# Channel shuffle on one core: the second load goes to ScalarE's queue, and the 16 KB tile moves from the last place to the third

## The chip, the core and the metric

The kernel runs on one core of a Trainium2 chip. The time is in device microseconds (us): the median of three runs, 316.16 us (316.13 to 316.22). One further view is the profile of a single execution, which took 316.22 us; its traced span is 314.4 us, and the 1.8 us between lie around the span. Of the engines only three matter here: SyncE (SP) and ScalarE (ACT), which issue the transfers between the chip's memory (HBM) and the core's on-chip memory (SBUF), and VectorE (DVE), which copies. The transfers are carried out by the core's 16 DMA engines.

## The reference

```python
batch, h, w, c = 16, 64, 64, 256      # x, float32; groups = 8
channels_per_group = c // groups      # 32
x = x.reshape(batch, h, w, groups, channels_per_group)
x = x.transpose(0, 1, 2, 4, 3)
x = x.reshape(batch, h, w, c)
```

Each of the 65,536 rows of 256 floats is permuted in the same way: read as an 8 x 32 matrix, it is written transposed. There is no arithmetic. 67.11 MB are read and 67.11 MB are written.

## The kernel before

The rows lie one behind the other in memory, 1 KB each. The kernel cuts them into tiles. A tile of "q KB" gives each of the 128 partitions q whole rows that lie one behind the other, so each partition's part is one contiguous piece of q KB in HBM and in SBUF; the tile holds q x 128 KB.

The list `_SLOTS` (line 12) gives the sizes and the order. An entry is one buffer's filling, and an entry with several numbers is one buffer that is loaded, copied and stored in several pieces, side by side in the buffer. Before the change it reads: one buffer with a 4 KB and an 8 KB piece, one with 28 KB, twelve with 38 KB, one with 16 KB. They sum to 512 KB a partition. All buffers have the size of the biggest entry, 38 KB.

There are two input buffers (`_IN_BUFS`) and three output buffers (`_OUT_BUFS`), taken in turn. For each entry the loop does three things. The loads of all its pieces are issued by SP (line 55). Then, piece by piece, VectorE copies from the input to the output buffer, and the copy's access pattern does the transposition (line 57), and ACT issues the store (line 61).

The order on each engine is the order of the program (the schedule is manual). What sets the pace between engines is the buffers. SP issues the first loads of the first two entries without waiting. The load of entry n waits until the copies of entry n-2 have all read their input buffer; SP's queue holds nothing else. A copy waits for its own load, and for the stores of entry n-3 to have left its output buffer. A store waits for its copy. SP's loads and ACT's stores stand in two DMA queues, called q1 and q10 in the profile, which the same 16 DMA engines serve. At the end SP waits for the last stores (line 94).

## Time and profile before

| What | Value |
|---|---|
| median of 3 runs | 316.16 us (316.13 to 316.22) |
| profiled execution, its own time | 316.22 us |
| its span | 314.4 us |
| VectorE busy | 119.0 us (38%), 16 copies |
| mean DMA rate over the span | 427 GB/s (134.22 MB) |
| copy of a 38 KB tile | 8.79 us (mean of 12) |
| copy of 28, 16, 8, 4 KB | 6.57, 3.87, 2.02, 1.09 us |
| load of a 38 KB tile, issue to landing | 37.0 us (median) |
| store of a 38 KB tile, issue to landing | 42.6 us (median) |
| load of 4, 8, 28, 16 KB, issue to landing | 3.3, 5.4, 14.7, 30.4 us |
| store of 4, 8, 28, 16 KB, issue to landing | 14.3, 25.0, 30.9, 15.2 us |

The busy times are per engine, over the span. The time from issue to landing runs from the instruction that issues a transfer to the last of its bytes; it includes the waiting behind earlier transfers of the same queue and the sharing of the DMA engines with the other queue, so it isn't the time that the transfer would take alone. In a timeline line the first number is the start in us from the span's start, the second the duration, and the square brackets hold the engine's idle time just before and what ended it.

### The profile page before, as it was taken

What the parts mean: (1) busy time and instruction counts of PE and PEld (TensorE: products, weight loads), DVE (VectorE), ACT (ScalarE), POOL (GpSimd) and SP (SyncE); (2) the same over time, 40 slices, a digit from 0 to 9 for tenths busy, and PEclk for the clock granted to TensorE, in tenths of its full rate; (3) what the DMA queues carried; (4) which work ended last, traced back from release to release, by engine and by line L of the source; (5) the groups of instructions that cost most, each with busy time, mean ns of one, the idle gap of its engine ahead of it and who ended that gap; (6) DMA issues with size and microseconds to landing.
All of it is one profiled execution on the core that took longest, in us unless ns stands there. A gap on an engine that the chain in (4) does not pass through costs nothing.

```text
span 314.4 us, 132 instructions
## 1 busy us (share of the span) xinstructions
DVE 119.0 (38%) x16; POOL 0.2 (0%) x4
## 2 busy tenths in 40 slices
DVE  2081907309109109019028028037046055065400
POOL 0000000000000000000000000000000000000000
DMA  7999999999999999999999999999999999999997
GB/s 317 405 441 416 435 416 483 401 465 406 450 421 446 426 436 436 401 470 396 475 396 475 396 470 401 470 401 470 401 450 421 446 426 436 436 417 450 429 421 321
DMA packets 4608, 134.22 MB, mean 427 GB/s; under 512 B 512, under 2 KB 512, under 8 KB 768
## 3 DMA queue, kind: packets, MB, share of 16 engines
q1 hardware_dynamic: 2304, 67.11, 49.8%
q10 hardware_dynamic: 2304, 67.11, 49.4%
HBM read 67.11 MB, written 67.11 MB: 427 GB/s over the span
## 4 chain that ended last, share of the span: by engine, by line
DMA 76%; DVE 19%; issue 0%; SPq 0%; DVEq 0%
DMA in_tile<-in_x_dram 76%; DVE out_tile L57 19%; SPq L55 0%; DVEq L57 0%
## 5 line engine op out<-in xcount | busy, mean ns | idle before, releaser
L57 DVE COPY out_tile<-in_tile 128x9728 f32<-128x9728 f32 (+4 forms) x16 | 119.0, 7440 | 179.4 <-DMA in_tile<-in_x_dram 179.4
L80 POOL MEMSET const-uint8-127<- 128x1 uint8 x1 | 0.1, 103 | 0.0
L80 POOL MEMSET const-bfloat16-1.0<- 128x1 bf16 x1 | 0.1, 102 | 0.0
L80 POOL MEMSET const-float32-1.0<- 128x1 f32 x1 | 0.1, 100 | 0.0
L80 POOL MEMSET const-float32-0.0<- 128x1 f32 x1 | 0.1, 99 | 0.2 <-issue 0.2
## 6 DMA issues: line engine op xcount, KB each, us to landing
in_tile<-in_x_dram SPq DMA_DIRECT2D x12, 4864.0 KB, 37.0
out_dram<-out_tile ACTq DMA_DIRECT2D x12, 4864.0 KB, 42.6
in_tile<-in_x_dram SPq DMA_DIRECT2D x1, 3584.0 KB, 14.7
out_dram<-out_tile ACTq DMA_DIRECT2D x1, 3584.0 KB, 30.9
in_tile<-in_x_dram SPq DMA_DIRECT2D x1, 2048.0 KB, 30.4
out_dram<-out_tile ACTq DMA_DIRECT2D x1, 2048.0 KB, 15.2
in_tile<-in_x_dram SPq DMA_DIRECT2D x1, 1024.0 KB, 5.4
out_dram<-out_tile ACTq DMA_DIRECT2D x1, 1024.0 KB, 25.0
```

Source lines behind the costliest of these rows:

```text
L57: nc.vector.tensor_copy(out=out_tile[:, cols].rearrange("p (i j g) -> p i j g", j=CPG, g=G), in_=in_tile[:, cols].rearrange("p (i g j) -> ...
L80: nc = _bacc.Bacc("TRN2", target_bir_lowering=False, num_devices=1)
```

## The change

Two things change. In the list of sizes the 16 KB tile is no longer an entry of its own at the end: it is the third piece of the first entry, behind 4 and 8 KB. The list has 14 entries instead of 15, with the same 16 pieces, and the last entry is now a 38 KB tile. The load of the 8 KB piece is issued by ACT, and all other loads by SP as before. The order on SP is now 4, 16, 28 KB, then twelve times 38 KB; on ACT it is the 8 KB load and then the stores of 4, 8, 16, 28 KB and twelve of 38 KB; on VectorE the copies run in the order of the stores. The first 38 KB load now waits for the copies of three pieces, the last of them the 16 KB one.

```diff
-_SLOTS = [[4, 8], [28]] + [[38]] * 12 + [[16]]
+_SLOTS = [[4, 8, 16], [28]] + [[38]] * 12
...
         for q, start, cols in pieces:
-            nc.sync.dma_start(out=in_tile[:, cols], in_=rows(x_flat, start, q))
+
+            queue = nc.scalar if q == 8 else nc.sync
+            queue.dma_start(out=in_tile[:, cols], in_=rows(x_flat, start, q))
         for q, start, cols in pieces:
             nc.vector.tensor_copy(
```

## The prediction

> **What bounds the kernel now.** I read the page first: the busy shares, the slices, the DMA queues.

> ```profile
> DVE 119.0 (38%) x16; POOL 0.2 (0%) x4
> ...
> DMA  7999999999999999999999999999999999999997
> ...
> q1 hardware_dynamic: 2304, 67.11, 49.8%
> q10 hardware_dynamic: 2304, 67.11, 49.4%
> ```

> The only compute engine is idle 62% of the time. The DMA engines are busy in every slice, and the loads (queue 1, issued by SP) and the stores (queue 10, issued by ACT) together fill 99.2% of their span. So the question for any edit is: does it make the DMA engines idle for longer or shorter, or does it change the bytes per microsecond? The chain of waits, read alone, would mislead: it puts 19% on VectorE, but while it walks through a copy another load and a store are moving. The timeline gives the rate. A copy that waits for its load starts as the load lands, so copy starts are load landings:

> ```profile
> 4.06 1.09 DVE L57 COPY out_tile<-in_tile 128x1024 f32<-128x1024 f32 x1 [4.06 <-DMA in_tile<-in_x_dram]
> 6.61 2.02 DVE L57 COPY out_tile<-in_tile 128x2048 f32<-128x2048 f32 x1 [1.46 <-DMA in_tile<-in_x_dram]
> 16.36 6.57 DVE L57 COPY out_tile<-in_tile 128x7168 f32<-128x7168 f32 x1 [7.73 <-DMA in_tile<-in_x_dram]
> ...
> 71.31 8.75 DVE L57 COPY out_tile<-in_tile 128x9728 f32<-128x9728 f32 x1 [13.40 <-DMA in_tile<-in_x_dram]
> ...
> 278.19 8.73 DVE L57 COPY out_tile<-in_tile 128x9728 f32<-128x9728 f32 x1 [14.21 <-DMA in_tile<-in_x_dram]
> 294.54 3.87 DVE L57 COPY out_tile<-in_tile 128x4096 f32<-128x4096 f32 x1 [7.62 <-DMA in_tile<-in_x_dram]
> ```

> From 71.31 to 278.19 nine 38 KB tiles land, and as many stores leave: 206.88 / 9 = 22.99 us for 2 x 38 = 76 KB a partition, or 0.3025 us per KB a partition. I call 1 KB a partition one unit. The whole kernel moves 512 units in and 512 out: 1024 x 0.3025 = 309.8 us of the 314.4 us span. Only 4.6 us lie outside. Of them 2.85 stand before and in the first landing (4.06 minus 4 x 0.3025 = 1.21), and 0.75 behind the last store's landing (298.45 issued, 15.2 to land, 313.65; span end 314.4). About 1 us is lost on the way. The head and one dip show in the table of stretches (columns: stretch, its length, DVE, POOL, clock, DMA share, GB/s):

> ```profile
> 1.50:2.00 0.50, 0.00 (x0) 0.00 (x0) 1.00 0.74 90
> 2.00:2.50 0.50, 0.00 (x0) 0.00 (x0) 1.00 0.45 164
> 2.50:5.00 2.50, 0.94 (x1) 0.00 (x0) 1.00 1.05 431
> ```

> ```profile
> 30.00:35.00 5.00, 4.82 (x1) 0.00 (x0) 1.00 0.93 369
> ```

> Against the steady 433 GB/s (134.22 MB in 309.8 us) the ramp from 1.5 to 2.5 loses 0.40 + 0.31 = 0.71 us, and the dip up to 5 x (1 - 369/433) = 0.74 us. From 2.5 us on the rate is already 431.

> **The change part by part.** The sum is made against the profiled execution, 316.22 us (span 314.4 and 1.8 around it); it is 0.06 above the median, 316.16. Bytes, DMAs (16 loads, 16 stores, same sizes) and copies are the same before and after; only queue and order change. I write L for a load, S for a store, with its KB a partition. After: SP issues L4, L16, L28, then twelve L38; ACT issues L8, then S4, S8, S16, S28, twelve S38.

> 1. *L8 goes from SP's second place to ACT's first.* An issue took 327 to 426 ns on SP. Does the second issue hold up data? No: L8 landed 2.55 us after L4 (6.61 - 4.06), and its 8 units are 2.42 us at the steady rate, so at most 0.13 us lay between two DMAs issued one behind the other. What can still change is the ramp, where two queues now fill at once. Bounds: a gain of all of it, -0.71, or that L8 pays a first-transfer ramp of its own, +0.71. I take 0, by the nearer row, the 2.55 us. [...]

> 2. *L4 and L8 share the engines.* Two queues do share: S4, 4 units or 1.21 us by itself, needed 14.3 us from issue to landing beside L28. So L4 can land anywhere from 4.06 (it goes first) to 6.6 (both finish together, same 12 units). The copies (1.09, 2.02) and S4, S8 start up to 2.5 us later: S4 issued at 7.7 instead of 5.19, S8 at 9.7 instead of 8.66. The cover is L16 and L28, already queued on SP without any wait: 44 units, 13.3 us of transfer behind the first 12. Cost 0. [...]

> 3. *L16 moves to third, into the first buffer.* L38's first load waits for that buffer, released by the 16 KB copy (3.87 us), no longer by the 8 KB one. L16 lands at 6.6 + 16 x 0.3025 = 11.4, or 12.7 with all of S4 mixed in; copy done at 15.3 to 16.6. On SP's queue L28 then still needs 8.5 us or more after L16's last byte, until 19.9 to 21.2. A DMA's start-up is about 1 us (first issue at 0.73, first bytes after 1.50). So the first L38 is ready by 17.6 at the latest, 2 to 3 us before L28 is through. Cost 0. Next: L28 lands by 23.5 (6.6 plus 16, 28, 4 and 8 units), its copy (6.57) ends by 30.1 and frees the other buffer for the second L38, while the first L38 runs to 31.4 at the earliest and to about 37 with the stores that share with it (S16 and the rest of S8). Cost 0, with the thinnest cover. Later loads are as before: each copy is idle 14.2 us before its tile lands, and that is the reserve.

> 4. *SP, ACT and DVE queues.* SP has one issue fewer ahead of the first waiting load and none at the end; ACT's L8 waits for nothing and stands ahead of stores that cannot be due before a copy. The two extra semaphore waits that a third piece brings fall on loads and stores that are long done. 0.

> 5. *The end: the last load is 38 KB, with a copy of 8.75 us and a store of 38 units (11.5 us) behind it, instead of 16 KB, 3.87 and 4.84.* This costs only if the store queue runs dry before the last store is issued. In the middle of the run S lands 42.6 us after its issue and the load issued at the same moment after 37.0 (the page's medians), so when the last load lands the store two tiles back has 5.6 us left at half rate, 2.8 alone, and the store of the tile before, issued 14.2 us earlier, is still whole: 11.5. That is 14.3 us of stores. The last store is ready after 8.75 + 0.36 (issue) + 1 = 10.1 us. Reserve 4.2 us, cost 0. Gain also 0: before, the engines stayed full after L16 had landed at 294.5 (the last two of the 40 slices move 421 and 321 GB/s, and the last holds the 0.75 us after the landing), so a shorter copy and store at the end had no gap to save. Fewer reads mixed in at the end changes little: the last 16 KB store landed 4.86 us behind the 38 KB one (313.65 - 308.79), against 4.84 at the mixed rate. Bounds for the end: 0 to +10.1.

> Sum: 316.22 + 0 + 0 + 0 + 0 + 0 = 316.2; on the median, 316.15.

> **The rivals.** (a) *Main case:* DMA-bound through, no difference beyond 0.2% (0.63 us, about what a measurement of this kernel can tell from no change). Small terms of the ramp of 0.3 either way: 315.8 to 316.5.
> (b) *A faster head.* The ramp fills from two queues, and the dip at 30 to 35, which stands where small and large stores meet, is gone in the new order. For it: both are real losses in the table. Against: L8 followed L4 without a gap, so the ramp isn't made by the second issue. Gains between 0.43 and 0.71 + 0.74: 314.7 to 315.7; it needs most of both to pass 0.2%.
> (c) *A slower head.* Two queues starting together make two ramps (+0.71), or a second dip comes, as there is one more small store ahead of the large ones (+0.74): 316.9 to 317.6. For it: the dip is unexplained. Against: from 35 to 280 none comes, whatever meets.
> (d) *A gap before the last store.* The DMA engines go idle between the store before last and the last. It decides once less than 10.1 us of stores are queued as the last load lands; each us under that is a us lost. If S38 did not lag at all, S11 would have run 14.2 us at half rate and leave 11.5 - 7.1 = 4.4: +5.7, 322. Against: the 42.6 us landings.

> **How the numbers follow.** (a) 0.74, (b) 0.11, (c) 0.10, (d) 0.05. A part of (b) ends inside 0.2%, as does a part of (a)'s own spread outside; they cancel. Faster 0.11, same 0.74, slower 0.15. The range leaves out (d), the far half of (c) and of (b): 315.5 to 316.9. Within the main case alone it would be 315.8 to 316.5.

> **What the profile after would show.** Right: 38 KB tiles landing every 23.0 us as before; DMA slices 9 throughout, the last too but for its end; the first copy later than 4.06, up to 6.3, with no loss; 16 KB landing at 11 to 13; span 314.0 to 314.8. The last copy starts near 314.4 - 0.75 - 11.5 - 14.3 = 288, and the last store needs more than 20 us to land; under 15 us means (d). Step 3 is wrong if SP's wait for the 16 KB copy ends after L28 has landed. I am wrong if the rate itself moves: 0.3% on the 0.3025 is 0.9 us, more than all the terms above.

## The result: 4% slower, and where the trace shows it

| | before | after |
|---|---|---|
| median, us | 316.18 (316.11 to 316.22, 6 runs) | 328.85 (326.95 to 330.98, 6 runs) |
| ratio | | 1.0406, 95% interval 1.0358 to 1.0454 |
| profiled execution, us | 316.22 | 330.98 |
| its span, us | 314.4 | 329.2 |

The prediction, no change and at most 316.9, was wrong by 12.7 us. Ratios here and below are over the executions within 1.5% of the fastest of their kernel, all at a granted clock of 1.00; where executions lie further above (e5, e8, e17), they are listed one by one. The page of the profile after, its busy shares, slices, queues and DMA issues:

```profile
DVE 119.3 (36%) x16; POOL 0.2 (0%) x4
...
DMA  8999999999999999999999999999999999998985
GB/s 317 437 427 410 428 430 433 436 433 426 388 430 397 430 397 416 402 430 383 421 426 392 411 426 402 407 421 407 440 383 416 421 411 397 435 430 383 454 359 217
...
q10 hardware_dynamic: 2448, 68.16, 51.4%
q1 hardware_dynamic: 2160, 66.06, 46.8%
...
in_tile<-in_x_dram SPq DMA_DIRECT2D x12, 4864.0 KB, 39.6
out_dram<-out_tile ACTq DMA_DIRECT2D x12, 4864.0 KB, 64.2
```

The DMA engines are as busy as before (slices of 9 up to the last few) and the copies cost the same (119.3 us, 119.0 before). So, but for the last few slices, nothing idles; the same bytes take longer in the DMA engines. The two queue lines say which bytes: a line's share times the span, over its MB, is the engine time that a MB of this queue took. Queue 1, loads only, takes 46.8% of 329.2 us for 66.06 MB, 2.33 us per MB; before it was 49.8% of 314.4 us for 67.11 MB, 2.33 as well. Queue 10, the stores and now the 8 KB load, takes 51.4% of 329.2 us for 68.16 MB, 2.48 us per MB; before, 49.4% of 314.4 us for 67.11 MB, 2.31. **The stores became about 7% dearer, the loads did not.**

The timeline of after, VectorE's copies and ACT's stores:

```profile
6.56 3.04 DVE L59 COPY out_tile<-in_tile 128x1024 f32<-128x1024 f32 x2 [6.56 <-DMA in_tile<-in_x_dram]
7.71 295.67 ACTq L63 DMA_DIRECT2D out_dram<-out_tile  x16
11.88 3.87 DVE L59 COPY out_tile<-in_tile 128x4096 f32<-128x4096 f32 x1 [2.28 <-DMA in_tile<-in_x_dram]
22.02 6.64 DVE L59 COPY out_tile<-in_tile 128x7168 f32<-128x7168 f32 x1 [6.27 <-DMA in_tile<-in_x_dram]
...
73.88 8.77 DVE L59 COPY out_tile<-in_tile 128x9728 f32<-128x9728 f32 x1 [11.64 <-DMA in_tile<-in_x_dram]
97.36 8.93 DVE L59 COPY out_tile<-in_tile 128x9728 f32<-128x9728 f32 x1 [14.72 <-DMA out_dram<-out_tile]
...
294.21 8.80 DVE L59 COPY out_tile<-in_tile 128x9728 f32<-128x9728 f32 x1 [15.16 <-DMA out_dram<-out_tile]
```

The head is as the prediction had it. From 73.88 to 294.21 nine tiles go through, 24.48 us each, where before it was 22.99: 9 x 1.49 = 13.4 of the 14.8 us between the two spans. The loss is spread evenly over the steady part. The table of stretches says the same (columns: stretch, its length, DVE, POOL, clock, DMA share, GB/s), first for after, then for before:

```profile
1.50:2.00 0.50, 0.00 (x0) 0.00 (x0) 1.00 0.66 98
2.00:2.50 0.50, 0.00 (x0) 0.00 (x0) 1.00 0.77 180
2.50:5.00 2.50, 0.00 (x0) 0.00 (x0) 1.00 0.96 382
30.00:35.00 5.00, 0.00 (x0) 0.00 (x0) 1.00 0.85 358
100.00:150.00 50.00, 17.97 (x3) 0.00 (x0) 1.00 1.00 408
150.00:200.00 50.00, 18.22 (x3) 0.00 (x0) 1.00 1.01 412
```

```profile
100.00:150.00 50.00, 20.66 (x3) 0.00 (x0) 1.00 1.01 436
150.00:200.00 50.00, 17.70 (x2) 0.00 (x0) 1.00 1.01 435
```

With a DMA share of 1.00 or 1.01 in both, 23 to 28 GB/s are missing. One more thing has changed, and it is the first suspect: copies now wait for stores to leave the output buffer. What VectorE waited for in after (us in total, times, longest):

```profile
DVE out_tile L59 <- DMA out_dram<-out_tile: 140.9, 9, 16.2
DVE out_tile L59 <- DMA in_tile<-in_x_dram: 42.8, 6, 11.6
```

**The packets.** Below the views of the profile, the trace holds a record of every packet that a DMA engine moved: start, duration, queue, size. A tile's DMA leaves eight data packets on each of the 16 engines, each as long as one partition's piece (38,912 bytes for a 38 KB tile), and a closing packet of 4 bytes, 7 to 9 ns long: nine turns (4608 packets for the 32 DMAs of before, and of after, 9 x 16 each). The record does not name the engine, but from 20 to 285 us each packet starts within 6 ns of where another one ended, in before and in after, so sixteen chains can be followed. In each chain the two queues alternate packet by packet. Written with L for load and S for store, a letter for the 38 KB tile (a is the first), and the packet's number 0 to 7 in its DMA (closing packets left out), the pattern in the middle of the run is

```
before, all 16 engines:   Lf4 Sd2 Lf5 Sd3 Lf6 Sd4 Lf7
after, 12 engines:        Ld0 Sa0 Ld1 Sa1 Ld2 Sa2 ...   Lg7 Sd7 Lh0 Se0
after, 4 engines:         Lf3 Sc5 Lf4 Sc6 Lf5 Sc7
```

Before, the store's number trails the load's by two; with nine turns on both sides this distance stays for the whole run. I call the store's number minus the load's, counted round nine, the *offset* (the expectations call it the phase): 7 before. After, it is 0 on twelve engines (store packet n goes right behind load packet n) and 2 on four. The durations of the 38 KB packets:

```
                      load      store
before                1439 ns   1439 ns
after, offset 0       1439 ns   1629 to 1658 ns (engines' means)
after, offset 2       1439 ns   1439 ns
```

Eight store packets that are 0.2 us longer make 1.6 us per tile on the twelve engines: about the 1.49 us that the timeline lost. Where does the offset come from? In after the first store is issued at 7.71 us and comes in just as the 16 KB load ends and the 28 KB load begins; twelve engines have "L16 packet 7, its closing packet, L28 packet 0, S4 packet 0, L28 packet 1, S4 packet 1", four took S4 two turns earlier, right behind L16 packet 7. Before, the first store was issued at 5.19 and came in behind packet 2 of the 28 KB load on all 16 engines. So the theory for the tests: **the change of order and queue itself is harmless; it moves the moment at which the first store meets the loads, this fixes an offset of 0, and at offset 0 the store packets are slow.** Rivals: the new order as such; the 8 KB load in ACT's queue; the copies' waits for stores; the distance of the addresses in HBM.

### The profile page after: what moved, and what is told of

It is laid out like the page before. It is cut to its first block, busy times and chain, and to the rows that moved or that the text cites. A ratio compares the mean times of both kernels' runs of the same rounds, so it can differ in the third digit from the quotient of the medians.

```text
span 329.2 us, 131 instructions
## 1 busy us (share of the span) xinstructions
DVE 119.3 (36%) x16; POOL 0.2 (0%) x4
## 2 busy tenths in 40 slices
DMA packets 4608, 134.22 MB, mean 408 GB/s; under 512 B 512, under 2 KB 512, under 8 KB 768
## 3 DMA queue, kind: packets, MB, share of 16 engines
q10 hardware_dynamic: 2448, 68.16, 51.4%
q1 hardware_dynamic: 2160, 66.06, 46.8%
HBM read 67.11 MB, written 67.11 MB: 408 GB/s over the span
## 4 chain that ended last, share of the span: by engine, by line
another core or an unknown queue 43%; DVE 31%; DMA 18%; issue 0%; DVEq 0%; SPq 0%
DVE out_tile L59 31%; DMA in_tile<-in_x_dram 18%; DVEq L59 0%; SPq L57 0%
## 5 line engine op out<-in xcount | busy, mean ns | idle before, releaser
L59 DVE COPY out_tile<-in_tile 128x9728 f32<-128x9728 f32 (+4 forms) x16 | 119.3, 7460 | 183.7 <-DMA out_dram<-out_tile 140.9
## 6 DMA issues: line engine op xcount, KB each, us to landing
out_dram<-out_tile ACTq DMA_DIRECT2D x12, 4864.0 KB, 64.2
```

Of the source, the lines that this page charges most:

```text
L59: nc.vector.tensor_copy(out=out_tile[:, cols].rearrange("p (i j g) -> p i j g", j=CPG, g=G), in_=in_tile[:, cols].rearrange("p (i g j) -> ...
```

## The experiments

All edits are to the kernel after, unless another is named.

**e1, e2: one half of the change at a time.** e1 has the new order with all loads on SP, e2 the old order with the 8 KB load on ACT.

```diff
 e1
-            queue = nc.scalar if q == 8 else nc.sync
+            queue = nc.sync
 e2
-_SLOTS = [[4, 8, 16], [28]] + [[38]] * 12
+_SLOTS = [[4, 8], [28]] + [[38]] * 12 + [[16]]
```

> The new order of tiles, with the 8 KB load back on SP. Three theories. P (phase): on 12 of the 16 DMA engines every store packet stands directly behind the load packet of the same number (first store packet behind the first load packet of a tile, and so on), and these store packets take 1.6 us instead of 1.44; the phase is set at the start, by how many load packets are through when the first store arrives. Q (queue): a load in ACT's queue ahead of the stores is the cause by itself. O (order): the three-piece first entry, or the 38 KB tile at the end, is the cause by itself. Here the 4 KB piece lands alone, its store is issued near 5.2 us, as before the change, and arrives amid the 16 KB load, not at the start of the 28 KB one. P: 315.8 to 316.8. Q: 316. O: 327 to 331.

> The old order of tiles (16 KB last), with the 8 KB load on ACT. P: the first store is issued near 7.7 us, as in the changed kernel, but the 28 KB load has then run since 6 us, so the store arrives in the middle of it: phase off by some packets, 315.8 to 316.8. Q: 327 to 331. O: 316.

e1: 316.34 us (316.21 to 316.45), ratio 1.0002 (0.9992 to 1.0011). e2: 317.03 us (316.27 to 317.35), ratio 1.0019 (1.0009 to 1.0028). Each half alone costs 0.0 to 0.2%, both together 4%; a sum of two costs is excluded. e2 lies a little above what P expected. In e1 the first store is issued at 5.19 and meets the 16 KB load, offset 5 on 15 engines and 4 on one; in e2 at 7.82, meeting the 28 KB load, offsets 4 and 5. The 38 KB store packets are 1439 ns on average in both.

**e3: the first store later.** The copy of the 4 KB piece is made three times, so that its store is issued about 2 us later.

```diff
-            nc.vector.tensor_copy(
+            for _ in range(3 if q == 4 else 1):
+                nc.vector.tensor_copy(
```

> The changed kernel whole, with the 4 KB copy made three times in a row (same result), which delays the first store by 2.2 us, about two packets of the 28 KB load, and removes nothing. P: the store now arrives two packets late, no packet of a store stands behind the load packet of its own number, 316 to 317, although work was added. Q and O: 327 to 331, as the delay is hidden.

Measured 318.18 us (316.15 to 318.54; one group of runs at 316.15 to 316.43, one at 318.15 to 318.54), ratio 1.0039 (1.0017 to 1.0061). More work, and 10 us faster. The first store is issued at 9.81, the offsets are 7 and 8, the store packets between 100 and 300 us take 1439 to 1446 ns (means over 20 us; the few slower ones are on the three engines at offset 8). The profiled execution is of the upper group, which lies above the 316 to 317 expected; what sets the two groups apart I did not find. Its waits and a stretch:

```profile
DVE out_tile L60 <- DMA out_dram<-out_tile: 148.4, 11, 14.6
```

```profile
100.00:150.00 50.00, 21.51 (x3) 0.00 (x0) 1.00 1.01 435
```

Here copies wait even more for stores than in after (148.4 against 140.9 us), at the full 435 GB/s. So the first suspect falls: the waits for the output buffer are a consequence of how far the stores lag (59.2 us from issue to landing here, 64.2 in after, 49.8 in e1, where no copy waits for a store), and can account for at most the 2 us by which this execution lies above before, not for 12.7.

**e4: other distances in HBM.** The 38 KB loads read 57 rows earlier, so the output holds other rows; the transfers have the same sizes.

```diff
-            queue.dma_start(out=in_tile[:, cols], in_=rows(x_flat, start, q))
+            queue.dma_start(out=in_tile[:, cols], in_=rows(x_flat, start - (57 if q == 38 else 0), q))
```

> The changed kernel with each 38 KB load reading from 57 rows (one and a half packets) earlier in memory; the data are then other rows, and the time is that of the same transfers. This keeps the order of packets and the partitions and moves only the distance in memory between what is read and what is written at the same time. P with the cause in memory addresses (read and write at a fixed, round distance): 316 to 320. P with the cause in the on-chip memory (store and load on the same partition at once), Q and O: 327 to 331.

Measured 327.15 us (326.45 to 328.08), ratio 1.0345 (1.0319 to 1.0370): still slow, with offset 0 on 15 engines and store packets of about 1.58 us. Moving the distance between the addresses read and written by 57 KB changes nothing, so a particular distance in HBM is not it.

**e5: slow without any load in ACT's queue.** e1 with the 4 KB copy made four times.

```diff
 against e1
-            nc.vector.tensor_copy(
+            for _ in range(4 if q == 4 else 1):
+                nc.vector.tensor_copy(
```

> The new order of tiles with all loads on SP, which ran like the kernel before, and now the 4 KB copy made four times in a row (same result): the first store is issued near 8.5 us instead of 5.2, so that it comes right behind the first packet of the 28 KB load, as in the changed kernel. P (phase): slow without any load in ACT's queue, 325 to 332, with store packets of 1.6 us. Rival (the load in ACT's queue is needed): 316 to 317.

Measured 317.35, 343.56, 347.15 and 347.87 us. Three are slow, as P expected, but by far more than it expected: in the profiled execution (347.15) four engines are at offset 0, with store packets of about 2.1 us between 100 and 160 us, and they fall far behind the twelve others, whose store packets are at 1439 ns there. So here four engines in the bad offset cost more than all 16 of them in e9 and e11 below (347.15 us against 327.86 and 327.55). One execution of the same program took 317.35; its packets were not recorded, so its offset is unknown.

**e6, e7: transfers in halves by partition, a miss.** All 38 KB transfers are made as two DMAs, partitions 0 to 63 and 64 to 127; e7 stores the upper half first. If "same partition" were the reason, e7 should be fast.

```diff
-            queue.dma_start(out=in_tile[:, cols], in_=rows(x_flat, start, q))
+            for half in (slice(0, 64), slice(64, P)) if q == 38 else (slice(0, P),):
+                queue.dma_start(out=in_tile[half, cols], in_=rows(x_flat, start, q)[half])
```

> The changed kernel with every 38 KB load and store made as two transfers, partitions 0 to 63 and then 64 to 127, in this order on both sides. A control for the next: store and load packets of the same number still name the same partition. If the slow packets come from store and load on one partition at once: 324 to 335, store packets about 1.6 us. More semaphores are shared here, so the phase can also be lost; then it tells nothing.

> As the control, but the stores go upper half first, the loads lower half first: packets of the same number now name partitions 64 apart, with all else in the same order. If the cause is one partition at once: 316 to 320. If it is the equal number or the rhythm of the two queues by itself: as slow as the control.

e6 took 436.82 us, e7 419.15 us. The load packets now take 2.3 us on average (2.2 in e7), and the rate drops, in e6 to:

```profile
DMA packets 4992, 134.22 MB, mean 309 GB/s; under 512 B 896, under 2 KB 896, under 8 KB 1152
```

Made of transfers of 64 neighbouring partitions, the kernel runs at 309 GB/s (321 in e7) where after has 408, which drowns the question. Why such transfers are slower, no run here shows.

**e8, e9: moving the offset by small means.** e8 stores only the 28 KB piece in two halves (one closing packet, so one turn, more on the store side). e9 copies the first 1 KB of the 4 KB piece twice, which moves the first store by 0.3 us.

```diff
 e8
+            for half in (slice(0, 64), slice(64, P)) if q == 28 else (slice(0, P),):
+                nc.scalar.dma_start(
+                    out=rows(out_flat, start, q)[half], in_=out_tile[half, cols]
+                )
 e9
+            if q == 4:
+                nc.vector.tensor_copy(
+                    out=out_tile[:, 0:c].rearrange("p (i j g) -> p i j g", j=CPG, g=G),
+                    in_=in_tile[:, 0:c].rearrange("p (i g j) -> p i j g", g=G, j=CPG),
+                )
```

> The changed kernel with one edit behind the start: the store of the 28 KB tile alone is made as two transfers of 64 partitions. The start is untouched, so the first store still meets the first packet of the 28 KB load. Two transfers have two closing packets instead of one, which moves all later stores by one place against the loads. P: 316 to 318. If the slowness has another cause in the start or in the order of tiles: 326 to 331.

> The changed kernel with a quarter of the 4 KB copy made once more ahead of it, about 0.3 us, so that the first store comes a little later still and more than 12 of the 16 engines begin it behind the first packet of the 28 KB load. If equal numbers alone make a store packet slow: 325 to 331 as before. If it also takes engines of another phase beside them (with 12, 15 and 4 engines in this phase the store packets took 1.64, 1.59 and up to 2.2 us): with all 16 in it the time falls to 316 to 319.

e8: 319.29, 320.46, 320.70 and 345.31 us; ratio of the three 1.0124 (1.0099 to 1.0150). Most of the loss is gone in three, though they stay above the 316 to 318 expected, and the halved store brings a disorder of its own. The one execution whose packets are seen is the 345.31: between 100 and 200 us one engine of the 16 is at offset 0 there, with store packets of 1.97 us, and the 15 others are at 1.44 to 1.46. e9: 327.86 us (325.81 to 328.29), ratio 1.0358 (1.0324 to 1.0392): all 16 engines at offset 0, store packets about 1.57 us. So a mixture of offsets among the engines, as in after, isn't needed for the loss.

**e10, e11: a pair that differs in the offset and in 64 KB.** One extra load, whose data nobody reads, goes ahead of the first 38 KB load: 64 partitions of 1 KB in e10, five turns; 128 partitions in e11, nine turns. Nine turns leave an offset counted round nine as it is, five shift it.

```diff
+        if parts == [38] and start_of_38 is None:
+            start_of_38 = first
+            extra = extra_pool.tile([P, c], F32, name="extra")
+            nc.sync.dma_start(out=extra[:64], in_=rows(x_flat, 0, 1)[:64])
 e11: [:128] in both places
```

> The changed kernel with one small transfer added: SP loads 64 rows (64 KB) into a tile of 64 partitions that nobody reads, between the 28 KB and the first 38 KB load. It gives each DMA engine four packets and a closing one more on the load side, and so moves all later loads by five places against the stores. P (phase): no store packet stands behind the load packet of its own number any more, 316 to 318 although work was added. Without the phase: as the changed kernel, 327 to 331.

> The control: the same transfer with 128 rows in 128 partitions. Each engine gets eight packets and a closing one, nine places, which is just the length of a tile's round, so the phase stays what it was. P: slow, 326 to 332. If any small transfer at this place helps, by a delay or otherwise: 316 to 318.

e10: 316.98 us (316.88 to 317.41), ratio 1.0029 (1.0017 to 1.0040). e11: 327.55 us (327.32 to 330.83), ratio 1.0385 (1.0336 to 1.0434). Waits and a stretch of e10, then of e11:

```profile
DVE out_tile L65 <- DMA in_tile<-in_x_dram: 175.8, 15, 14.3
```

```profile
100.00:150.00 50.00, 19.51 (x3) 0.00 (x0) 1.00 1.00 433
```

```profile
DVE out_tile L65 <- DMA in_tile<-in_x_dram: 191.4, 15, 15.5
```

```profile
100.00:150.00 50.00, 17.70 (x2) 0.00 (x0) 1.00 1.00 411
```

```
e10, all 16 engines:  Lf2 Sc7 Lf3 Lf4 Sd0      (offset 5)  store packets 1439 ns
e11, all 16 engines:  Le7 Sc7 Lf0 Sd0 Lf1      (offset 0)  store packets 1575 to 1586 ns
```

e11 moves 64 KB more than e10, 0.05% of the whole, and takes 10.6 us longer. Its loads are at 1439 ns as in e10, and its store packets alone are longer; with e1 to e9, this leaves the offset as the cause. e11 also clears three bystanders: its copies wait for loads alone, its stores run two tiles behind the loads (three in after), and all engines are alike; it is slow all the same.

**e12 to e14: even and odd partitions, inconclusive.** Why is offset 0 slow: because both packets belong to the same partition, or because of the place in the rhythm? To tell, load and store must keep their numbers and differ in the partition. Taking even partitions first and then odd ones hardly loses rate: e12, which is e1 with all 38 KB transfers split so, took 316.78 us (316.48 to 319.60), ratio 1.0029 (1.0001 to 1.0056). e13 is e9 split so on both sides, e14 stores the odd ones first.

```diff
+            for odd in (0, 1) if q == 38 else (None,):
+                half = slice(None) if odd is None else slice(odd, None, 2)
+                queue.dma_start(out=in_tile[half, cols], in_=rows(x_flat, start, q)[half])
...
+            for odd in (0, 1) if q == 38 else (None,):      # e14: (1, 0)
+                half = slice(None) if odd is None else slice(odd, None, 2)
+                nc.scalar.dma_start(
+                    out=rows(out_flat, start, q)[half], in_=out_tile[half, cols]
+                )
```

> The kernel with all loads on SP (phase free, 316.3 us) with the same even and odd split on both sides: the price of the split by itself. All theories: store packets 1.44 us; total 316 to 320 if transfers of every second partition run at the full rate.

> The kernel with the extra quarter copy (all 16 engines in the slow phase), and every 38 KB load and store made as two transfers of 64 partitions, the even and then the odd ones, on both sides alike. Four packets and a closing one each, so packets of the same number are still of the same partition. Partition theory: store packets near 1.58 us, slow. Rhythm theory (two closing packets meeting makes all packets slow): slow too. This is the control.

> The same, but the stores go odd partitions first, the loads even first: the rhythm is unchanged, packets of the same number are now of neighbouring partitions. Partition theory: store packets 1.44 us, total near that of the free run. Rhythm theory: as slow as the control.

e13: 318.71 us (318.60 to 318.71); e14: 318.17 us (318.04 to 318.25). Both fast, the control too, because the offset 0 was lost in both: the split 38 KB loads have ten turns each while the stores of 8 and 16 KB beside them still have nine, and the halves of the third 38 KB load then come late besides (in e13 VectorE is idle for 20.89 us ahead of that copy, 8.84 ahead of the one before). The offset is 2 ahead of that load and no longer 0 behind it. The pair tells nothing about the partition.

**e15, e16: the same on a base that holds the offset.** e11, split only from the fifth 38 KB load and the third 38 KB store on. These two run beside each other, so both sides go from nine turns to ten at the same place. e16 stores the odd partitions first.

```diff
-    for parts in _SLOTS:
+    for tile_no, parts in enumerate(_SLOTS):
...
+            for odd in (0, 1) if tile_no >= 6 else (None,):
+                half = slice(None) if odd is None else slice(odd, None, 2)
+                queue.dma_start(out=in_tile[half, cols], in_=rows(x_flat, start, q)[half])
...
+            for odd in (0, 1) if tile_no >= 4 else (None,):      # e16: (1, 0)
+                half = slice(None) if odd is None else slice(odd, None, 2)
+                nc.scalar.dma_start(
+                    out=rows(out_flat, start, q)[half], in_=out_tile[half, cols]
+                )
```

> The kernel of e11 (all 16 engines with the store's packet number equal to the load's), but from the fifth 38 KB load and the third 38 KB store on each transfer is two DMAs, first the even partitions, then the odd ones. In e11 that load runs beside that store, so both sides go from 9 turns a tile to 10 at the same place and the numbers stay equal. Control for the next run. Both theories: slow, 326 to 329 us, split store packets near 1.58 us. If the split itself breaks the pattern, 317 to 321, and then the pair tells nothing.

> As e15, but the split stores take the odd partitions first. The turns and their numbers are the same as in e15; only the store's packet now belongs to a partition next to the one that the load's packet just filled, never to the same. Theory 'same partition': the split store packets are back at 1.44 us; only the two tiles ahead of the split are slow, 318 to 321 us. Rival 'same place in the rhythm' (what counts is the turn, not the partition): as slow as e15, 326 to 329.

e15: 328.88 us (328.01 to 329.46), ratio 1.0410 (1.0392 to 1.0427): the control is slow, as both theories expected. e16: 319.93 us (317.86, 319.03, 320.84, 321.06), ratio 1.0113 (1.0069 to 1.0157). The three upper times are what "same partition" expects, but the profiled execution is the lowest, and its packets show an offset of 2 already in the head: it had escaped before the swap came, and proves nothing.

**e17, e18: both cases in one execution.** Now the store's order is swapped in only a part of the run: in e17 from the seventh 38 KB store on, in e18 up to the sixth. The rest is e15.

```diff
 e17
+            for odd in (1, 0) if tile_no >= 8 else (0, 1) if tile_no >= 4 else (None,):
 e18
+            for odd in (0, 1) if tile_no >= 8 else (1, 0) if tile_no >= 4 else (None,):
```

> In the profile of e16 the engines had fallen into another offset between store and load already in the head, before the swap, so its fast packets prove nothing; its other executions, whose packets are not seen, took 319 to 321 us. This run puts both cases into one execution. As e15 (load and store split, even partitions first on both sides, numbers equal), but from the seventh 38 KB store on, which runs beside the ninth 38 KB load, the store takes the odd partitions first. Turns and numbers stay as they are. 'Same partition': if the head locks into equal numbers, the store packets take about 1.58 us up to the sixth 38 KB store and 1.44 us from the seventh on, 6 slow tiles of 10: 323 to 325.5 us. 'Same place in the rhythm': 1.58 us on both sides of the swap, 328 to 329.5.

> The mirror image: odd partitions first on the third to the sixth 38 KB store, even partitions first (as the loads) from the seventh on. 'Same partition': slow for the two tiles ahead of the split, 1.44 us from the third to the sixth 38 KB store, slow again from the seventh to the tenth, 323 to 325.5 us, if the head locks into equal numbers. 'Same place in the rhythm': 1.58 us from the first 38 KB store on, 328 to 329.5.

e17: 317.83, 317.90, 324.57 and 324.75 us; the profiled one is 317.83 and had again escaped in the head (offset 2 on all engines), the two upper ones lie where "same partition" put them, but their packets were not recorded. e18: 323.26, 323.56, 323.94 and 327.91 us (the last lies just under the 328 to 329.5 of the other theory, and its packets were not recorded); its profiled execution, 323.26, had the offset 0 from the start on 15 engines and 2 on one. Stretches of e15, all of it even-even, then of e18, in which the first lies in the swapped part and the second behind it:

```profile
135.00:185.00 50.00, 19.36 (x3) 0.00 (x0) 1.00 1.00 411
...
225.00:275.00 50.00, 17.80 (x2) 0.00 (x0) 1.00 1.00 414
```

```profile
135.00:185.00 50.00, 20.30 (x3) 0.00 (x0) 1.00 1.01 433
...
225.00:275.00 50.00, 18.89 (x3) 0.00 (x0) 1.00 1.00 413
```

And the 38 KB store packets over time, the mean of all 16 engines' packets in 20 us, which needs no assignment to engines (us from the span's start, ns):

```
from       80   100   120   140   160   180   200   220   240   260
e15      1596  1584  1580  1587  1583  1585  1584  1578  1581  1578
e18      1581  1498  1444  1442  1439  1439  1509  1574  1575  1572
```

In e18 the packets in the middle, at the time of the swap, read like this on 15 engines (e even, o odd partitions):

```
Lfo1 Sde1 Lfo2 Sde2 Lfo3 Sde3 Lge0 Seo0      store packets 1439 ns
```

The numbers are still equal and the turns are those of e15, but the store's packet belongs to a neighbour of the partition that the load's packet has just filled. The slowness goes as the swap begins and comes back within half a tile of its end (the first half of the seventh store is at 1465 ns on average, the second at 1574). So it is not the place in the rhythm: **in the steady part a 38 KB store packet was slow when it read the partition that the load packet just ahead of it on the same engine wrote to (1574 ns in e18, 1439 when it read a neighbour).** The record names no partitions; that packets of one number belong to one partition follows from load and store having the same shape, and the swap bears it out. The swap also moves the distance in HBM by one piece of 38 KB; e4 moved it by 57 KB and stayed slow.

What stays open: why the store packet is slow in this pairing; why the pairing alone is not enough at first; and why a packet takes 1.58 us with all engines in it, 1.64 with twelve, 2.1 with four and 1.97 with one. The pairing stands from the first store on, but in the six profiled executions with 12 engines or more at offset 0 the slowness sets in only while the third 38 KB load runs, 58 to 77 us into the span, whichever store is then beside it: in after, e4 and e9 it is the 28 KB store (up to 1415, 1399 and 1539 ns in place of 1062), in e11, e15 and e18 the first 38 KB store, from its fifth or sixth packet on (the 28 KB store is at 1062 throughout).

## Why the prediction was wrong

- *The rate of 0.3025 us per unit.* This is the step that failed. It was read from before as a property of the bytes ("same bytes, same DMAs") and kept for after. It was a property of the bytes and of how the two queues interleave: after, it is 24.48 / 76 = 0.322 us. The last sentence of the prediction named the case ("if the rate itself moves") and gave it no chance and no place in the range; none of the rivals (b), (c), (d) contains it.
- *Step 1, the 8 KB load on ACT: 0.* Right in kind, a little off in size, within its bounds of 0.71 either way. From 2.5 to 5.0 us the head moved 382 GB/s where before it was 431, and the first 28 units were in by 11.88 us, where 2.85 + 28 x 0.3025 = 11.32 would have been without loss: about 0.6 us lost. The runs with the 8 KB load on ACT and no collision, e2 and e10, agree: 317.03 and 316.98, about 0.9 us slower than before in the same rounds (316.17 and 316.11; e10 includes half a unit of extra load, 0.15 us). What it left out is that the move delays the first store, from 5.19 to 7.71 us; step 2 said so and costed the delay at nothing, since it looked only for data made late.
- *Step 2: 0.* The first copy started at 6.56, just past the predicted 6.3 of the list of signs and within the 6.6 of the step. In the trace the two queues take turns packet by packet: a turn is one partition's piece, up to 38,912 bytes and 1439 ns (1629 to 1658 ns for the stores at offset 0). I weighed the sharing for the first 2.5 us alone; the turns go on for the other 320 as well.
- *Step 3, the buffer release: 0.* Held. The 16 KB tile landed at 11.88 (predicted 11.4 to 12.7), the 28 KB one at 22.02 (by 23.5), and the first 38 KB load was not late.
- *Step 4, the queues: 0.* It asked what waits behind an issue, not which transfer a store meets when it arrives. It also miscounted, at no cost: SP has three issues ahead of the first waiting load before and after (4, 8, 28 and 4, 16, 28 KB). "The extra semaphore waits fall on transfers long done" isn't what cost the time: e1 has the same order and is at 316.34.
- *Step 5, the end: 0.* Held on the twelve engines that end last: no gap before the last store. The last copy starts at 294.21, not 288, which is the lost rate, and the last store takes 25.4 us to land, over 20 as it would without a gap. The four engines at offset 2 are ahead by then: they stand idle for about 2.2 us until the last store's packets come at 303.9, and are done at 315.5, when the others work on to between 325 and 328. So the slow engines set the time.
- *Rivals.* (b) did not occur; no run shows a gain of its 0.43, the longest issue on SP: with the 8 KB load on ACT, e2 and e10 were about 0.9 us slower. (c), the slower head at 316.9 to 317.6, is where e2 and e10 lie, so without the collision it would probably have been right and the main case just missed (e10 less its extra load is at 316.8, between the two); after also has a dip (358 GB/s at 30 to 35, 369 before). (d) occurred only on the four engines that were not the last, so it cost nothing.
- *Waits for stores.* Not foreseen: with stores 64.2 us from issue to landing (42.6 before), the output buffers became the releasers of the copies. e3 has these waits at the full rate, and e11 the loss without them.

## What to carry to other kernels

In this kernel, where loads and stores of the same shape run side by side in two queues, the DMA engines locked them into a fixed pairing of packets that the arrival of the first store decided, and a pairing of the same partition cost 3.3% (316.98 against 327.55 us by an extra load of 64 or 128 partitions). So a change in the head of a DMA-bound kernel is not judged by the head's microseconds: compare the queues' busy time per MB before and after (here 2.31 and 2.48 us for the stores, 2.33 both times for the loads), and if one queue has become dearer at a full DMA share, look at the packets. In these runs the pairing was moved by shifting the first store by about 2 us (e3, offsets 7 and 8; the 0.3 us of e9 were too little) or by adding five turns (e10, offset 5); e1, the new order with all loads on SP, is such a repair and equals the kernel before (316.34 against 316.17 us), it does not beat it.
